# A decoder layer in split f32 on one core: branch B's gate by a seven-product scheme behind v, ua beside the attention stages, branch A's gate whole beside the last heads

## The chip, the core and the metric

The kernel runs on one core of a Trainium2 chip. The metric is the device time of one execution, in microseconds (us). Three runs of the kernel before gave 615.21, 615.33 and 616.19 us, a median of 615.33. The profiles are of one execution each. The engines are called PE (matrix products), PEld (the loads of PE's stationary operand), DVE, ACT and POOL (the three that work on vectors); SP only issues transfers.

## The reference, cut to what matters

One layer, 512 tokens, 1024 channels. A single projection of x gives nine pieces; branch A is a gated mixing of tokens within chunks of 128, branch B an attention with two softmax maps for each of 8 heads.

```python
h = x @ w_in
ua, va, za, qh, kh, vh, zb, ga, gb = jnp.split(h, IN_OFFSETS, axis=-1)

ua = gelu(ua)
va = layer_norm(gelu(va), a_ln_g, a_ln_b)
vc = va.reshape(bn, n_chunks, CHUNK, A_GROUPS, A_GROUP_DIM)
sa = einsum("gts,bnsgc->bntgc", tril(a_w_s), vc) + a_b_s.T[:, :, None]
ya = ua * sa.reshape(bn, s_len, A_WIDTH) * silu(za)

o = diff_attention(rope(qh) * dk ** -0.5, rope(kh), vh, lam)     # 8 heads, two maps each
yb = rms_norm(o, b_subln_g) * (1.0 - lam_init) * silu(zb)

merged = sigmoid(ga) * (ya @ w_branch_a) + sigmoid(gb) * (yb @ w_branch_b)
ple = sigmoid(x @ w_ple_gate) * (p @ w_ple)
return layer_norm(alpha * x + merged @ w_out + ple, ln_g, ln_b)
```

## The kernel before

**Products.** Every f32 operand of a projection is kept as a high part and the remainder (`xh` and `xl` of x, `wh` and `wl` of a weight tile), and one f32 product is three matmuls: high by high, high by low, low by high (`three`, L292). A "product" below is one such matmul, of a stationary 128 x 128 piece by a moving 128 x 512 piece. Weights arrive as raw tiles of 512 KB (128 x 1024, "wr" or "wa"). ACT copies a tile into `wh` (L410), and DVE subtracts that from the raw tile into `wl` (L413).

**Two ways to make 1024 output columns.** The plain way is a group for each 128 features (`feature_group`, L465): eight steps of three products, 24 in all, into one PSUM bank, so 192 for 1024 columns. The other is `quad` (L650), which multiplies the blocks of a 2 x 2 split by seven products of blocks instead of eight: seven steps of 24 products, 168 in all, from sums of blocks of x and sums of blocks of the weights. The sums of weights are made in one of two ways. In a chain (`CHAINS`) the raw tile of a step becomes that of a later step when POOL issues a transfer that adds another weight block to it (`follow`, L385), behind DVE's last read. Or the sums lie ready in DRAM, made earlier by `make_sums` at the points of `READY_MADE`.

**The order.** PE's matmuls are written out in order. `product` (L280) counts them, and `later(n, fn)` puts the work of the other engines n products behind the point at which it is called. So a table of small numbers says beside which product each piece of ACT, DVE, POOL, PE and DMA work is issued; every engine then takes its own instructions in that order. The stages, with their products:

1. kq (96): k and q of heads 0 and 1. Then zb's first pair of feature groups (48), kept in two banks, and v as a quad (168).
2. Three stages of 144: k, q and zb of the next pair of heads (48 each); `attention(p - 1)` for the pair before lies between the products, and `gate_b` puts Silu of zb into `yb`.
3. `attention(3)` beside ua (192, L1050) and the first two groups of za (48, L1079; `HELD`).
4. va as a quad of ready sums (168), then **zq**: the other six groups of za as a narrow quad. It has features on the rows and blocks of three groups, so its 252 matmuls have 256 columns, and its tiles 768 used columns.
5. ga, gb, pg, ple, wb, wa and out. The norm of va (`va_norm`: statistics on DVE, a power on POOL, then `centre` and `shift` of 128 x 1024 on DVE) is issued in zq and ga, by `NORM`; branch A's spatial products (`spatial`, PE, followed by two DVE operations) by `SPATIAL`, 32 products apart.

**A head.** `scores` (L796) takes two of the "sc" banks for a block of queries; DVE reduces each into `p`, ACT takes the exponential, DVE combines the two maps, PE transposes and multiplies by v into the one bank "po" (`values`). The tail of a head is `squares` (DVE and ACT), `norm` (DVE, then POOL's power), `scale` (POOL) and `turned` (PE transposes the head, DVE multiplies the bank by a constant and by `yb`, L888), by `TAIL` products behind the last values. `PERIOD` is the distance of the blocks, `stretch` multiplies it.

Of the kernel before, what the change touches and what calls it, by code (L numbers as in the profile page):

```python
# [21 lines left out]
P = 128  # L22
# [17 lines left out]
EARLY_ASK = ("k", "q", "zb")  # L40
# [6 lines left out]
SWAP = 132  # L47
BEGIN = 14
STRETCH = 1.0
# [4 lines left out]
TAIL = (2, 14, 28, 48)  # L54
NORM = (2, 112, 270, 330)
SPLITS = {'va': ((0, 10), (13, 16)), 'wb': ((4, 7), (13, 16)), 'zq': ((1, 4), (10, 17)), '': ((0, 4), (6, 12))}
BEHIND = (8, 14)
LAST = (7, 11)
GELU = 10
SILU = (20,)  # L60
CENTRE = (12, 24)
SPATIAL = (390, 32)
READY_MADE = {'va': (2, 6, 50, 32, 140, 174, 260, 314), 'wb': (162, 290, 170, 318, 356, 470), 'zq': (320, 430, 434, 538), 'ga': (540, 566), 'gb': (752, 786), 'pg': (612, 745), 'wa': (1500, 1570)}
# [5 lines left out]
FIRST_GATE = 168  # L69
SUMS_OF_X = (60, 75, 84, 84, 150, 152, 174, 179)  # L70
XS = (24, 14, 98, 18)
AUX = (124, 136, 104, 130, 130)
# [4 lines left out]
GOES_ON = ('v', 'gb', 'pg', 'wb', 'wa')  # L77
HELD = 2
BLOCKS = 3
NARROW = 2 * BLOCKS * P  # L80
# [44 lines left out]
def narrow_units(off):  # L125
    return [("n", off + c * BLOCKS * P, kk) for c in range(2) for kk in range(4)]


# [10 lines left out]
PART_READY = {'zq': (0, 2), 'ga': (2,), 'gb': (2,), 'wb': (0, 1, 2), 'pg': (2,), 'wa': (2,)}  # L139
# [6 lines left out]
def plan():  # L146
# [68 lines left out]
def pack(ws):  # L215
    out = np.empty((len(UNITS), P, 1024), np.float32)
    for i, (w, u) in enumerate(UNITS):
# [8 lines left out]
        elif u[0] == "n":  # L226
            _, c, kk = u
            s = a[2 * kk * P:(2 * kk + 2) * P, c:c + BLOCKS * P]
            out[i, :, :NARROW] = s.reshape(2, P, BLOCKS * P).transpose(1, 0, 2).reshape(P, NARROW)
            out[i, :, NARROW:] = 0.0  # L230
# [16 lines left out]
def hybrid_layer(ctx: ExitStack, tc: tile.TileContext, a, out: bass.AP):  # L247
# [79 lines left out]
    def weights(unit, n=1024):  # L327
        return (W[unit] if isinstance(unit, int) else wsd[unit[0]][unit[1], unit[2]])[:, :n]

    def width(name):  # L330

        return NARROW if name == "zq" else 1024

    def make_sums(name, at):

        cols = width(name)
        there = wsd[name][:, :, :, :cols]

        def step(n, what, of, j):
            source = weights((name, of, j) if isinstance(of, int) else MADE_OF[name, of][j], cols)  # L340
# [10 lines left out]
    def load(u, cuts=(0, 1024), first=(sp,)):  # L351
# [15 lines left out]
        cuts = [min(n, width(STEPS[u][0])) for n in cuts]  # L367
# [5 lines left out]
    def follow(u):  # L373
# [6 lines left out]
        else:  # L380
# [3 lines left out]
            n = width(STEPS[u][0])  # L384
            pool.dma_start(out=raw[u][:, :n], in_=weights(STEPS[FOLLOWS[u]][1], n), accum_op=OP.add)  # L385
# [7 lines left out]
    def prep(u, cuts=(0, 1024)):  # L393
        if u < len(STEPS) and u not in split:
            run(load(u))
            h, l = parts_of(u)
            cuts = [min(n, width(STEPS[u][0])) for n in cuts]
# [5 lines left out]
    def spread(u, high=HIGH[0], low=LOW[0]):  # L403
# [3 lines left out]
        h, l = (part[:, :width(STEPS[u][0])] for part in parts_of(u))  # L407

        def high_part():
            act.activation(h, raw[u][:, :width(STEPS[u][0])], AF.Copy)  # L410

        def low_part():
            dve.tensor_tensor(out=l, in0=raw[u][:, :width(STEPS[u][0])], in1=h.bitcast(F32), op=OP.subtract)  # L413
            follow(u)
# [18 lines left out]
    def next_pair(name, i):  # L433
# [7 lines left out]

        pace = BLOCKS / 2 if name == "zq" else 1

        def ask(at, v, fits=lambda chain: True):
            if not pumping and v < len(STEPS) and fits(STEPS[v][2]):
                later(round(at * pace), lambda: run(load(v)))
# [8 lines left out]
        for j, at in enumerate(SPLITS.get(name, SPLITS[""])):  # L455

            at = BEHIND if i == 5 and j and name not in SPLITS else LAST if i == 6 and j else at
            spread(u + 2 + j, *(round(pace * n) for n in at))
# [191 lines left out]
    def quad(name, left, banks, place, done):  # L650
# [4 lines left out]
        if name == "zq":  # L655
            X, Y, Z = ([bank[:, :(2 - t) * 2 * P] for t, bank in enumerate(two)] for two in banks)
        kept = {}

        def keep(key, bank):
            kept[key] = tmp[0](key[0])[:, :bank.shape[-1]]  # L660
# [16 lines left out]
        def after2(t):  # L677
            if goes_on:
                z = place(0, t)
                return done(0, t, tmp[0]("s1")[:, :X[t].shape[-1]] if z is None else z, X[t])  # L680
# [18 lines left out]
        def after4(t):  # L699
            z = place(0, 2 + t)  # L700
            done(0, 2 + t, tmp[0]("z")[:, :Y[t].shape[-1]] if z is None else z, Y[t])
# [3 lines left out]
        for i, (bank, first, after) in enumerate(steps):  # L705
            w = next_pair(name, i)
            for t in range(2):
                if name == "zq":
                    for j, k in ((j, k) for j in range(2 - t) for k in range(4)):
                        h, l = w[k // 2]  # L710
                        m = slice(((k % 2) * BLOCKS + 2 * t + j) * P, ((k % 2) * BLOCKS + 2 * t + j + 1) * P)
                        three(bank[t][:, j * 2 * P:(j + 1) * 2 * P], h[:, m], l[:, m], *left[i](None, k),
                              first and k == j == 0, k == 3, True)
                else:
                    for k in range(4):
                        h, l = w[k // 2]
                        m = slice((k % 2) * T, (k % 2 + 1) * T)
                        three(bank[t], *left[i](t, k), h[:, m], l[:, m], first and k == 0, k == 3, True)
# [63 lines left out]
    def gate_b(p, banks, at):  # L782
        for bank in banks:
            feature_group(bank, "zb", xh, xl)

        def out_of():
            for i, bank in enumerate(banks):
                act.activation(yb[0][:, 2 * p + i, :], bank, AF.Silu)

        later(at, out_of)  # L790


    def attention(p, begin, stretch=1.0):
# [87 lines left out]

        def turned(h):
# [4 lines left out]
            z = yb[0][:, h, :]  # L887
            dve.scalar_tensor_tensor(out=z, in0=tr, scalar=g08[:, 0:1], in1=z, op0=OP.mult, op1=OP.mult)  # L888

        at = begin  # L890
        for hd in range(2):
# [9 lines left out]
            for d, fn in zip(TAIL, (squares, norm, scale, turned)):  # L901
# [76 lines left out]
    gate_b(0, (pbank("tr", 1), pbank("po", 1)), FIRST_GATE)  # L978

    ua = big.tile([P, KT, T], F32, name="ua", tag="U")  # L980

    def ua_out(g, bank):
        act.activation(ua[:, g, :], bank, AF.Copy)

    def ua_groups(groups):
        for g in groups:
            bank = pp()
            feature_group(bank, "ua", xh, xl)
            later(2, ua_out, g, bank)

    yb = []

    def place_yb():
        yb.append(big.tile([P, NH, T], F32, name="yb", tag="Y"))
# [4 lines left out]
    def v_done(c, t, z, source):  # L999
        if source is not z:  # L1000
# [3 lines left out]
    later(FIRST_GATE - 1, place_yb)  # L1004
    quad("v", operands(xh, xl, [of_piece(j) for j in range(4)]),
         ([pp(), pp()], [pbank("sc", 2) for _ in range(2)], [pp(), pbank("tx", 1)]), place_v, v_done)
    sums.clear()
    for name, at in READY_MADE.items():
        make_sums(name, at)
    for p in range(1, 4):  # L1010
# [3 lines left out]
        gate_b(p, (pp(), pp()), GATE)  # L1014
# [35 lines left out]
    ua_groups(range(KT))  # L1050

    def ua_gelu(g):
        act.activation(ua[:, g, :], ua[:, g, :], AF.Gelu)

    def za_groups(groups):
        def gate_a(g, bank):
            sz = bp.tile([P, T], F32, name="sz", tag="sz", bufs=4)

            def silu(source):
                act.activation(sz, source, AF.Silu)  # L1060
# [429 lines left out]
```

## Time and profile before

| | before |
|---|---|
| median of 3 runs | 615.33 us |
| the profiled execution | 615.15 us |
| its span | 613.4 us, so 1.75 us lie outside it |
| mean granted clock of PE | 0.997 |
| instructions | 8568 |
| HBM read, written | 121.05 MB, 32.64 MB: 251 GB/s over the span |

The profile gives busy times by engine, the span in 40 slices, the chain of waits that ended last, groups of instructions by line and tile, and the windows of any stretch. Busy times of neighbouring matmuls overlap, since the matmuls are pipelined; the distance of two starts is what one costs in a stream. A row of the timeline is: start in us, duration in us, engine, line, operation, out<-in, shape, and in brackets the idle time before it with what ended that.

### The profile page before, as it was taken

Reading aid. Unit: us, or ns where it says so; the run is one execution under the profiler, and the core shown is the slowest. Engines: PE = TensorE matmul, PEld = TensorE weight load, DVE = VectorE, ACT = ScalarE, POOL = GpSimd, SP = SyncE. Lnnn points to the kernel's source line nnn. Section 1 sums busy time; section 2 is a strip of 40 time slices with the busy share of each in tenths; the row PEclk is TensorE's granted clock in tenths of the full one; section 3 lists DMA queues with packets and bytes.
Section 4 is the critical chain, followed back from the end, with each engine's and each line's share of the span. In section 5 each row is a group of like instructions: output and inputs, shape, how many; then the busy total and the mean of one; then the engine's idle time right before and its main releaser. Section 6 shows DMA issues by size and latency. Waiting matters only on the chain.

```text
span 613.4 us, 8568 instructions
## 1 busy us (share of the span) xinstructions
PE 605.1 (99%) x3012; PEld 510.1 (83%) x3012; DVE 464.5 (76%) x776; ACT 342.3 (56%) x537; POOL 121.5 (20%) x133
## 2 busy tenths in 40 slices
PE   9999999999999999999999999999999999999995
PEld 6888888888888888888889988888888888888884
DVE  6995677879879865856669878668787887879476
ACT  6656565564555564458656665555676464555310
POOL 1234002332422512220012111131220011110011
PEclk9999999999999999999999999999999999999998
DMA  8689889779697599559897899886989578998002
GB/s 309 221 245 182 251 297 241 261 208 309 240 241 284 186 262 299 126 180 283 258 336 197 217 243 233 251 199 186 291 236 316 172 192 245 243 251 310 30 34 104
DMA packets 45983, 140.62 MB, mean 229 GB/s; under 512 B 6100, under 2 KB 7252, under 8 KB 45588
## 3 DMA queue, kind: packets, MB, share of 16 engines
q1 hardware_dynamic: 35876, 106.38, 48.8%
q0 software_dynamic: 9488, 33.30, 29.9%
q8 instruction: 24, 0.39, 0.3%
q10 hardware_dynamic: 576, 0.39, 0.2%
q14 instruction: 19, 0.16, 0.1%
HBM read 121.05 MB, written 32.64 MB: 251 GB/s over the span
## 4 chain that ended last, share of the span: by engine, by line
PE 99%; DVE 0%; DVEq 0%; issue 0%
PE ps_pp L281 58%; PE ps_sc L281 19%; PE ps_tx L281 9%; PE ps_sc L802 3%; PE ps_po L847 3%; PE ps_tr L836 1%; PE ps_po L281 1%; PE ps_tr L281 1%; PE ps_po L485 1%; PE ps_tr L1173 1%; PE ps_po L1173 1%; PE ps_tx L886 0%; PE ps_po L1360 0%; PE ps_tr L1360 0%; DVE base L1402 0%; DVEq L1486 0%
## 5 line engine op out<-in xcount | busy, mean ns | idle before, releaser
L413 DVE TENSOR_TENSOR wl<-wr,wh 128x1024 fp32r<-128x1024 f32 (+1 forms) x143 | 177.8, 1250 | 39.3 <-ACT wh L410 39.0
L410 ACT ACTIVATE wh<-wr 128x1024 fp32r<-128x1024 f32 (+1 forms) x143 | 146.3, 1033 | 68.4 <-PE ps_pp L281 17.1
L281 PE MATMUL ps_pp<-xh,wh 128*128 128x512 f32 (+1 forms) x276 | 109.6, 398 | 0.0
L281 PE MATMUL ps_pp<-xl,wh 128*128 128x512 f32 (+1 forms) x276 | 107.3, 389 | 0.0
L281 PE MATMUL ps_pp<-xh,wl 128*128 128x512 f32 (+1 forms) x276 | 105.6, 383 | 0.0
L385 POOL DMA_DIRECT2D wr<-in_w x32 | 27.7, 876 | 181.0 <-DVE wl L413 127.0
L815 ACT ACTIVATE p<-p,sth 128x128 f32<-128x128 f32 (+3 forms) x64 | 35.5, 556 | 46.6 <-DVE sth L813 46.5
L281 PEld LDWEIGHTS ps_pp<-xh,wl 128*128 128x128 f32 x276 | 52.2, 189 | 8.8
L281 PEld LDWEIGHTS ps_pp<-xh,wh 128*128 128x128 f32 x276 | 52.3, 190 | 8.5 <-ACT wh L307 0.5
L281 PEld LDWEIGHTS ps_pp<-xl,wh 128*128 128x128 f32 x276 | 52.2, 189 | 8.2 <-DVE xl L308 0.4
L281 PE MATMUL ps_pp<-wh,xl 128*128 128x512 f32 (+1 forms) x144 | 55.4, 384 | 0.0
L281 PE MATMUL ps_pp<-wl,xh 128*128 128x512 f32 (+1 forms) x144 | 55.3, 384 | 0.0
L281 PE MATMUL ps_pp<-wh,xh 128*128 128x512 f32 (+1 forms) x144 | 55.2, 383 | 0.0
L747 POOL TENSOR_TENSOR hl<-m,hl 128x512 fp32r<-128x512 f32 x16 | 25.2, 1637 | 54.3 <-ACT hl L742 54.3
L809 DVE CUSTOM_DVE_ANT_0 p<-ps_sc,mask 128x128 f32<-128x128 f32 (+3 forms) x64 | 30.9, 483 | 6.4 <-PE ps_sc L802 6.3
L281 PE MATMUL ps_sc<-wl,xsh 128*128 128x512 f32 x88 | 34.4, 391 | 0.0
L281 PE MATMUL ps_sc<-wh,xsh 128*128 128x512 f32 x88 | 34.3, 390 | 0.0
L281 PE MATMUL ps_sc<-wh,xsl 128*128 128x512 f32 x88 | 34.2, 389 | 0.0
L281 PEld LDWEIGHTS ps_pp<-wl,xh 128*128 128x128 f32 x144 | 27.1, 188 | 5.3
L281 PEld LDWEIGHTS ps_pp<-wh,xl 128*128 128x128 f32 x144 | 27.1, 188 | 5.2
L281 PEld LDWEIGHTS ps_pp<-wh,xh 128*128 128x128 f32 x144 | 27.1, 188 | 5.2
L281 PE MATMUL ps_pp<-wh,xsl 128*128 128x512 f32 x80 | 31.2, 390 | 0.0
(321 smaller groups left out, 1280.8 us busy)
## 6 DMA issues: line engine op xcount, KB each, us to landing
wr<-in_w SPq DMA_DIRECT2D x81, 512.0 KB, 5.2
wr<-in_w POOLq DMA_DIRECT2D x28, 512.0 KB, 7.1
k<-hl SPq DMA_DIRECT2D x16, 256.0 KB, 5.5
q<-hl SPq DMA_DIRECT2D x16, 256.0 KB, 4.2
ws_va<-in_w POOLq DMA_DIRECT2D x8, 512.0 KB, 10.5
wr<-ws_va SPq DMA_DIRECT2D x8, 512.0 KB, 4.1
wa<-in_w POOLq DMA_DIRECT2D x6, 512.0 KB, 7.1
kx<-hl SPq DMA_DIRECT2D x12, 256.0 KB, 5.6
```

The lines of the kernel that those rows point to most:

```text
L281: pe.matmul(ps, s, m, start=start, stop=stop, skip_group_check=read_within)
L385: pool.dma_start(out=raw[u][:, :n], in_=weights(STEPS[FOLLOWS[u]][1], n), accum_op=OP.add)
L410: act.activation(h, raw[u][:, :width(STEPS[u][0])], AF.Copy)
L413: dve.tensor_tensor(out=l, in0=raw[u][:, :width(STEPS[u][0])], in1=h.bitcast(F32), op=OP.subtract)
L485: pe.matmul(idle, zeros[:, :P], zeros, start=True, stop=True)
L747: pool.tensor_tensor(out=hl[:, 3 - j, :], in0=m[2 * j], in1=hl[:, j, :].bitcast(F32), op=OP.subtract)
L802: pe.matmul(sc[m][:, :n], q[:, m, i * P:(i + 1) * P], kk[:, m, :n], start=o == 0, stop=o == 1)
L809: dve.tensor_tensor_reduce(out=pr[m][:, :n], in0=sc[m][:, :n], in1=mask[:, T - n:], scale=-(DK ** -0.5), scalar=3e38, op0=OP.add, op1=OP.m ...
L815: act.activation(pr[m][:, :n], pr[m][:, :n], AF.Exp, bias=st[:, m:m + 1], scale=-1.0, accum_out=st[:, 2 + m:3 + m])
L836: pe.transpose(tr[:, j * P:(j + 1) * P], ad[:, j * P:(j + 1) * P], ident)
L847: pe.matmul(po[:, i * P:(i + 1) * P], at[:, j * P:(j + 1) * P], v[:, j, h * P:(h + 1) * P], start=j == 0, stop=j == i)
L1173: pe.matmul(sa[:, t * P:(t + 1) * P], va[:, t, g * P:(g + 1) * P], aux[0][:, 0, g, :], start=True, stop=True)
```

## The change

- **zb** is one quad (168 products) right behind v, from the same sums of x. Its seven products end in tokens by features, Silu goes straight into `yb` (tag U). The chains of its weights are as v's.
- **ua** takes zb's place: pair 0 in two banks behind kq, pairs 1 to 3 in the three attention stages (`ua_pair`, Gelu from the bank). It moves from tag U to tag Y.
- **The gate of a head** is multiplied in before the turn: `gated` (DVE, `on` by `yb`) is a new step of the tail, between `scale` and `turned`; ACT then copies the turned bank into `yb`, scaled by the constant. The last head has a tail of its own (`LAST_TAIL`).
- **za** is eight plain groups (192) beside `attention(3)`, whose blocks come closer (`STRETCH` 0.78). Groups 0 to 4 are copied out of their bank and get Silu later (`SILU`), the last three at once. zq, its narrow tiles and all code for them go.
- **va** takes the banks in another order; the four norms of va are issued in ga (`NORM` 174, 224, 276, 326 from va's start), and the spatial products in gb, 17 apart. The points of the ready-made sums, of x's sums and of the norm's constants move: ga takes pg's, pg takes zq's.

```diff
-EARLY_ASK = ("k", "q", "zb")
+EARLY_ASK = ("k", "q", "ua")
-STRETCH = 1.0
+STRETCH = 0.78
 PERIOD = (13, 16, 20, 23)
-TAIL = (2, 14, 28, 48)
-NORM = (2, 112, 270, 330)
+TAIL = (2, 14, 26, 44, 56)
+LAST_TAIL = (2, 10, 20, 32, 42)
+SILU = (122, 5)
+NORM = (174, 224, 276, 326)
-SPATIAL = (390, 32)
+SPATIAL = (194, 17)
...
-GOES_ON = ('v', 'gb', 'pg', 'wb', 'wa')
+GOES_ON = ('v', 'zb', 'gb', 'pg', 'wb', 'wa')
...
     add("kq", "in", [("c", cols, kk) for kk in range(4)])
-    add("zb", "in", feature_units(ZB, 2))
+    add("ua", "in", feature_units(UA, 2))
     quad("v", "in", token_units(VO))
+    quad("zb", "in", token_units(ZB))
     for p in range(1, 4):
         add("k", "in", rope_units(KO, p))
         add("q", "in", rope_units(QO, p))
-        add("zb", "in", feature_units(ZB + 2 * p * P, 2))
-    add("ua", "in", feature_units(UA, KT))
-    add("za", "in", feature_units(ZA, HELD))
+        add("ua", "in", feature_units(UA + 2 * p * P, 2))
+    add("za", "in", feature_units(ZA, KT))
     ready_quad("va", "in", token_units(VA))
-    quad("zq", "in", narrow_units(ZA + HELD * P))
...
+        def gated(h):
+            on, _ = todo["sq", h]
+            dve.tensor_tensor(out=on, in0=on, in1=yb[:, h, :].rearrange("p (i d) -> p i d", i=NT), op=OP.mult)
+
         def turned(h):
...
-            z = yb[0][:, h, :]
-            dve.scalar_tensor_tensor(out=z, in0=tr, scalar=g08[:, 0:1], in1=z, op0=OP.mult, op1=OP.mult)
+            act.activation(yb[:, h, :], tr, AF.Copy, scale=g08[:, 0:1])
...
-            for d, fn in zip(TAIL, (squares, norm, scale, turned)):
+            for d, fn in zip(TAIL if h < NH - 1 else LAST_TAIL, (squares, norm, scale, gated, turned)):
...
+    def zb_done(c, t, z, source):
+        act.activation(yb[:, 4 * c:4 * c + 4, t * P:(t + 1) * P], source.rearrange("p (h d) -> p h d", h=4), AF.Silu)
+
+    one, two = [pp(), pp()], [pp(), pbank("tx", 1)]
+    quad("zb", of_pieces, (two, [pbank("sc", 2) for _ in range(2)], one), lambda c, t: None, zb_done)
...
+    def keep_z(g, bank):
...
+        act.activation(z, bank, AF.Copy)
+        later(SILU[0] + SILU[1] * g - clock[0] + began, gate_a, g, z, z)
+
+    def gate_a(g, z, source):
+        act.activation(z, source, AF.Silu)
+        later(4, times, g, z)
+
+    began = clock[0]
     for g in range(KT):
-        later(GELU + 2 * g, ua_gelu, g)
-    za_groups(range(HELD))
-    flush(8)
+        bank = pp()
+        feature_group(bank, "za", xh, xl)
+        if g < 5:
+            later(2, keep_z, g, bank)
+        else:
+            later(2, gate_a, g, bp.tile([P, T], F32, name="sz", tag="sz", bufs=3), bank)
+    flush(14)
...
-    quad("va", of_x, pairs(False), lambda c, t: va[:, t, c * T:(c + 1) * T], va_done)
     for t in range(NT):
         later(NORM[t], va_norm, t)
+    quad("va", of_x, ([pp(), pp()], [pbank("sc", 2) for _ in range(2)], [pp(), pbank("tx", 1)]),
+         lambda c, t: va[:, t, c * T:(c + 1) * T], va_done)
     for g in range(KT):
         later(SPATIAL[0] + SPATIAL[1] * g, spatial, g)
-    quad("zq", of_x, pairs(True), lambda c, t: None, za_done)
```

The order of the instructions at three places follows. First PE's queue at the end of va. Before, va's last matmuls stand ahead of zq's first:

```order
L281 MATMUL ps_pp<-wh,xh 128x512
L281 MATMUL ps_pp<-wl,xh 128x512
L281 MATMUL ps_pp<-wh,xl 128x512
L281 MATMUL ps_pp<-xh,wh 128x256
L281 MATMUL ps_pp<-xl,wh 128x256
L281 MATMUL ps_pp<-xh,wl 128x256
```

After, on the same engine at the same place, ga's first matmuls follow va's last:

```order
L268 MATMUL ps_sc<-wh,xh 128x512
L268 MATMUL ps_sc<-wl,xh 128x512
L268 MATMUL ps_sc<-wh,xl 128x512
L268 MATMUL ps_pp<-wh,xh 128x512
L268 MATMUL ps_pp<-wl,xh 128x512
L268 MATMUL ps_pp<-wh,xl 128x512
```

The 252 matmuls of 256 columns are gone from this place; the columns that they made stand in the stage before va.

Second, DVE's queue behind the last values of the last head (`on` is the head, `xt` a sum of x for va, `ss` and `ok` the sums of squares). Before:

```order
L856 TENSOR_TENSOR on<-ps_po,r0h 128x512
L858 TENSOR_SCALAR on<-on 128x512
L413 TENSOR_TENSOR wl<-wr_2640,wh 128x1024
L1043 TENSOR_TENSOR xt<-xt 128x2x256
L868 TENSOR_REDUCE ss<-sq 128x4
L869 TENSOR_SCALAR ok<-ss 128x4
L870 TENSOR_SCALAR ss<-ss 128x4
L872 TENSOR_SCALAR ss<-ss 128x4
L1043 TENSOR_TENSOR xt<-xt 128x2x256
L413 TENSOR_TENSOR wl<-wr_2711,wh 128x1024
L1043 TENSOR_TENSOR xt<-xt 128x2x256
L888 SCALAR_TENSOR_TENSOR yb<-ps_tr,g_123,yb 128x512
```

After, on the same engine behind the same values (`ua` by `sz` is branch A's gate):

```order
L824 TENSOR_TENSOR on<-ps_po,r0h 128x512
L826 TENSOR_SCALAR on<-on 128x512
L392 TENSOR_TENSOR wl<-wr_2877,wh 128x1024
L1006 TENSOR_TENSOR xt<-xt 128x2x256
L836 TENSOR_REDUCE ss<-sq 128x4
L837 TENSOR_SCALAR ok<-ss 128x4
L838 TENSOR_SCALAR ss<-ss 128x4
L840 TENSOR_SCALAR ss<-ss 128x4
L1014 TENSOR_TENSOR ua<-ua,sz 128x512
L1006 TENSOR_TENSOR xt<-xt 128x2x256
L392 TENSOR_TENSOR wl<-wr_2962,wh 128x1024
L852 TENSOR_TENSOR on<-on,yb 128x512
```

The gate's multiply now stands on DVE ahead of PE's transposes, where before a multiply stood behind them, and a product of branch A's gate lies in the tail.

Third, DVE's queue in ga, at the two blocks that are made from the "sc" banks (`s_` tiles). Before:

```order
L666 TENSOR_TENSOR s_3842<-ps_sc,s_3842 128x512
L666 TENSOR_TENSOR s_3864<-ps_sc,s_3864 128x512
L413 TENSOR_TENSOR wl<-wr_3296,wh 128x1024
L666 TENSOR_TENSOR s_3758<-s_3758,ps_pp 128x512
L413 TENSOR_TENSOR wl<-wr_3374,wh 128x1024
L1179 TENSOR_TENSOR y<-ps_po,aux 128x512
```

After, on the same engine at the same two blocks:

```order
L1106 BN_STATS vst<-va 128x6 x2
L1093 BN_AGGR mv<-vst 128x2
L1094 TENSOR_SCALAR mv<-mv 128x1
L392 TENSOR_TENSOR wl<-wr_3476,wh 128x1024
L641 TENSOR_TENSOR s_3673<-ps_sc,s_3673 128x512
L1110 SCALAR_TENSOR_TENSOR va<-va,mv,a_ln_g 128x1024
L641 TENSOR_TENSOR s_3696<-ps_sc,s_3696 128x512
L392 TENSOR_TENSOR wl<-wr_3277,wh 128x1024
L1114 SCALAR_TENSOR_TENSOR va<-va,rs,a_ln_b 128x1024
L641 TENSOR_TENSOR s_3589<-s_3589,ps_pp 128x512
```

One of va's four norms now stands among the blocks and the weight subtractions of ga's middle; before, the first spatial product's operations came there and the norms stood earlier.

More of the change, by code (lines that the diff above doesn't have):

```diff
@@ L383, in follow @@
                 home[FOLLOWS[u]] = home.pop(u)
-            n = width(STEPS[u][0])
-            pool.dma_start(out=raw[u][:, :n], in_=weights(STEPS[FOLLOWS[u]][1], n), accum_op=OP.add)
+            pool.dma_start(out=raw[u], in_=weights(STEPS[FOLLOWS[u]][1]), accum_op=OP.add)
     def parts_of(u):
@@ L457, in next_pair @@
             at = BEHIND if i == 5 and j and name not in SPLITS else LAST if i == 6 and j else at
-            spread(u + 2 + j, *(round(pace * n) for n in at))
+            spread(u + 2 + j, *at)
         return split.pop(u), split.pop(u + 1)
@@ L654, in quad @@
         X, Y, Z = banks
-        if name == "zq":
-            X, Y, Z = ([bank[:, :(2 - t) * 2 * P] for t, bank in enumerate(two)] for two in banks)
         kept = {}
         def keep(key, bank):
-            kept[key] = tmp[0](key[0])[:, :bank.shape[-1]]
+            kept[key] = tmp[0](key[0])
             act.activation(kept[key], bank, AF.Copy)
@@ L707, in quad @@
             for t in range(2):
[L708 to L718, printed above, removed]
+                for k in range(4):
+                    h, l = w[k // 2]
+                    m = slice((k % 2) * T, (k % 2 + 1) * T)
+                    three(bank[t], *left[i](t, k), h[:, m], l[:, m], first and k == 0, k == 3, True)
                 if after:
@@ L977, in hybrid_layer @@
     rope("q", 0, first_kq[2:], TURN_Q, STACK)
[L978 to L994, printed above, removed]
+    first_ua = ua_pair(0, (pbank("tr", 1), pbank("po", 1)))
     def place_v(c, t):
@@ L1013, in hybrid_layer @@
         rope("q", p)
-        gate_b(p, (pp(), pp()), GATE)
+        later(GATE, ua_pair(p, (pp(), pp())))
     attention(3, BEGIN, STRETCH)
```

105 lines of the change are left out of this document (35 added, 70 removed).

## The prediction

> **What bounds the kernel now.** I read the engine table, the slices and the chain of waits first.
>
> ```profile
> PE 605.1 (99%) x3012; PEld 510.1 (83%) x3012; DVE 464.5 (76%) x776; ACT 342.3 (56%) x537; POOL 121.5 (20%) x133
> PE   9999999999999999999999999999999999999995
> PEclk9999999999999999999999999999999999999998
> PE 99%; DVE 0%; DVEq 0%; issue 0%
> ```
>
> TensorE (PE) is busy for 605.1 us of the span of 613.4, in every slice but the last. Its granted clock is in the top tenth until the last slice, and the chain that ended last is 99% PE. So the time is the sum of the matmuls' own time, and a change is worth the matmuls that it takes out, less the waits it makes. What a matmul costs I read from the starts in PE's timeline at three stage borders: va's first, zq's first, ga's first.
>
> ```profile
> 281.36 0.39 PE L281 MATMUL ps_pp<-wh,xh 128*128 128x512 f32 x1
> 319.44 0.28 PE L281 MATMUL ps_pp<-xh,wh 128*128 128x256 f32 x1
> 349.67 0.40 PE L281 MATMUL ps_pp<-wh,xh 128*128 128x512 f32 x1
> ```
>
> va holds 168 matmuls of 512 columns in 319.44 - 281.36 = 38.08 us, **0.2267 us** each. zq holds 252 of 256 columns in 349.67 - 319.44 = 30.23 us, **0.1200 us** each. The printed durations (0.39, 0.28) overlap, and only the distance of the starts counts. Then the windows by stage; the columns are PE, its weight loads, DVE, ACT and POOL busy, the clock, the DMA share and GB/s.
>
> ```profile
> 42.00:76.00 34.00, 34.00 (x152) 28.15 (x151) 22.60 (x28) 21.00 (x27) 7.68 (x8) 1.00 0.91 222
> 122.00:168.00 46.00, 46.00 (x249) 39.11 (x246) 38.45 (x98) 25.70 (x57) 16.02 (x15) 1.00 0.81 253
> 214.00:281.00 67.00, 67.00 (x350) 56.71 (x349) 42.01 (x108) 38.88 (x77) 15.01 (x17) 1.00 0.78 215
> 319.40:349.70 30.30, 30.30 (x254) 30.26 (x254) 25.83 (x35) 20.13 (x30) 5.24 (x8) 1.00 0.82 228
> 349.70:388.00 38.30, 38.30 (x175) 31.84 (x174) 30.08 (x36) 23.07 (x30) 7.93 (x9) 1.00 0.92 234
> ```
>
> They are v, an attention stage, the last attention stage, zq and ga. PE idles in none, though DVE reaches 38.45/46.00 = 84% in an attention stage and 25.83/30.30 = 85% in zq. That is the level known to be harmless.
>
> **The sum of the matmuls.** zb goes from 8 groups of 24 products (192) to one seven-product quad (168): -24 of 512 columns. za goes from two groups held (48) to eight (192): +144. zq's 252 go. ua keeps its 192. So +120 x 0.2267 = +27.20, and -252 x 0.1200 = -30.23: **-3.03 us**. Both prices are elapsed time between starts, so nothing hidden is left to come out of them.
>
> The Trainium skill has another price: "TensorE: Matmul & The Clock Gate", section "Wait — 56ns, not 53.3ns?", gives N / 2.4 + about 2.5 ns for warm back-to-back matmuls. That is 215.7 and 109.2 ns, and the sum would be 120 x 0.2157 - 252 x 0.1092 = -1.63 us, an estimate from that page. The trace's 227 and 120 ns speak against it on both sizes.
>
> **Weights.** zq's half-filled tiles become full ones.
>
> ```profile
> L413 DVE TENSOR_TENSOR wl<-wr,wh 128x768 fp32r<-128x768 f32 x14 | 13.3, 953 | 3.3 <-ACT wh L410 3.3
> L413 DVE TENSOR_TENSOR wl<-wr,wh 128x1024 fp32r<-128x1024 f32 (+1 forms) x143 | 177.8, 1250 | 39.3 <-ACT wh L410 39.0
> ```
>
> The number of tiles that are split stays at 151; 14 subtractions take 1.25 instead of 0.95 us: +4.2 us on DVE, spread over the first half, beside PE. Nothing on the path.
>
> **zb's quad** needs the raw tile of one step to become the next one's by an accumulating transfer, as in v.
>
> ```profile
> 55.93 0.85 POOL L385 DMA_DIRECT2D wa<-in_w  x1 [2.79 <-DVE wl L413]
> 57.78 0.85 POOL L385 DMA_DIRECT2D wa<-in_w  x1 [1.01 <-DVE wl L413]
> wr<-in_w SPq DMA_DIRECT2D x81, 512.0 KB, 5.2
> wa<-in_w POOLq DMA_DIRECT2D x6, 512.0 KB, 7.1
> ```
>
> There are six more of these on POOL's queue, issued by the same rule as v's six, behind DVE's last read of the tile. v ran so with PE busy 34.00 of 34.00 us at a DMA share of 0.91. I take **0**. The nearest bad end is one tile that lands late by the difference of the two kinds of transfer, 7.1 - 5.2 = 1.9 us: range 0 to 1.9. In the other direction nothing can be gained, since PE did not wait here.
>
> **The gate in front of the turn.** Each head gains a DVE multiply by yb before PE's transposes; the multiply of the bank behind them (L888) becomes a copy on ACT. For a head in the middle I read where POOL's scale, DVE and PE stand.
>
> ```profile
> 210.66 1.04 POOL L880 TENSOR_TENSOR on<-on,f 128x512 f32<-128x512 f32 x1
> 212.33 0.75 DVE L827 SCALAR_TENSOR_TENSOR p<-p,rho,p 128x512 f32<-128x512 f32 x1
> 213.45 0.39 PE L886 MATMUL ps_tx<-ident,on 128*128 128x128 f32 x2
> 214.09 0.75 DVE L888 SCALAR_TENSOR_TENSOR yb<-ps_tx,g,yb 128x512 f32<-128x512 f32 x1 [1.01 <-PE ps_tx L886]
> ```
>
> The scale ends at 211.70, 1.75 us before the transposes at 213.45. The new multiply's turn comes 12 products, or 12 x 0.2267 = 2.7 us, ahead of them; the chain between is one operation of 0.75 behind at most one or two of that size. I take **0**; uncovered it would be 0.75 for each of 7 heads, 5.2 us. On DVE itself the multiply takes the place of L888.
>
> **The last head** is the tight one, since the end of the stage is its chain.
>
> ```profile
> 266.36 1.05 PE L847 MATMUL ps_po<-v,at 128*128 128x128 f32 x8
> 267.51 0.69 DVE L856 TENSOR_TENSOR on<-ps_po,r0h 128x512 f32<-128x512 f32 x1 [4.98 <-PE ps_po L847]
> 268.23 0.43 DVE L858 TENSOR_SCALAR on<-on 128x512 f32<-128x512 f32 x1
> 268.58 1.22 DVE L413 TENSOR_TENSOR wl<-wr,wh 128x1024 fp32r<-128x1024 f32 x1
> ...
> 270.31 0.68 DVE L868 TENSOR_REDUCE ss<-sq 128x4 f32<-128x512 f32 x1
> ...
> 271.68 1.41 POOL L873 TENSOR_TENSOR f<-ss,mhalf 128x4 f32<-128x4 f32 x1 [15.56 <-DVE ss L872]
> 273.17 0.22 POOL L874 TENSOR_TENSOR f<-f,ok 128x4 f32<-128x4 f32 x1
> 273.47 1.36 POOL L880 TENSOR_TENSOR on<-on,f 128x512 f32<-128x512 f32 x1
> 278.15 0.60 PE L886 MATMUL ps_tr<-ident,on 128*128 128x128 f32 x4
> ```
>
> From the start of the last values' last matmuls (about 267.0, in the row that ends at 267.41) to the scale's end at 274.83 are 7.8 us, and the transposes came 3.3 us later. Now the multiply (0.69) and a handover of some 0.1 make it 8.6; between the two points stand 39 products and the turn of the last values, about 39 x 0.2267 + 0.2 = 9.0 us. Margin **0.4 us**, so cost 0. Here, though, DVE has the products of ua with za's gate (eight of 0.69, two before) in the same stretch: one of them that falls ahead of the reduction takes the margin and 0.3 us more. I take **+0.2** for this and for all small waits together; range 0 to 1.25, one weight subtraction.
>
> The stage shrinks from 240 products to 192. Its own attention matmuls are 67.00 - 240 x 0.2267 = 12.6 us, so it will last 192 x 0.2267 + 12.6 = 56.1. DVE's work is 42.01 + 6 x 0.69 less two subtractions (2.5) = 43.7, or 78%, below the 84% above.
>
> **The norm of va** now lies whole in ga: before, two of the four were in zq.
>
> ```profile
> L1156 DVE BATCH_NORM_STATS2 vst<-va 128x6 f32<-128x512 f32 x8 | 5.1, 682 | 0.0
> L1160 DVE SCALAR_TENSOR_TENSOR va<-va,mv,a_ln_g 128x1024 f32<-128x1024 f32 x4 | 5.1, 1278 | 0.0
> L1164 DVE SCALAR_TENSOR_TENSOR va<-va,rs,a_ln_b 128x1024 f32<-128x1024 f32 x4 | 5.1, 1277 | 0.0
> ```
>
> One is 2 x 0.68 + 1.28 + 1.28 = 3.9 us. ga's DVE goes from 30.08 to about 30.08 + 2 x 3.9 = 37.9, less the one pair of branch A's spatial products that moves to gb (1.4): **36.5 of 38.1, 96%**. No stretch of the old kernel is so full. Weights are split some 20 products, 4.5 us, ahead of their use; behind a centre or shift and a block this leaves about 0.7 us at the narrowest (four operations, 1.23 + 0.69 + 1.28 + 0.69 = 3.9). So I still take 0, with 0 to 1.3 as range (one operation more ahead). The spatial products 17 instead of 32 apart put two DVE operations (1.4) and 1.3 weight splits into 3.9 us of gb: 77%, harmless.
>
> **Sum.** 615.15 (the profiled run; 613.4 of it the span, and 0.18 below the median of 615.33) - 3.03 + 0.2 = **612.3**.
>
> **Rivals.**
> A. *DVE is late in ga or in the last stage.* For: 96% and a margin of 0.4. Against: nowhere above did an 84% stage stop PE, and DVE may run ahead of its due points. Two places of up to 1.25 us, less the 0.2 counted, with the centre at 1.7: **614.0** (613 to 616).
>
> B. *The short matmuls were worth only half a long one.* 252 x 0.1133 = 28.56 us would be their own time, and the other 1.67 us of zq's 30.23 a wait for weights: the loads are busy 30.26 of 30.30, and the splitting engines may have caught up there. Without that pause the wait comes back in another stage, and the swap frees 28.56 - 27.20 = 1.36 us: **613.8**. Against: PE itself is busy 30.30 of 30.30 there, and va and ga run for 38 us each with no such pause. (The skill's page above stands for this one, with its 1.63.)
>
> C. *Slower: score banks.* The last two heads' blocks begin after 10, 13, 16, 18 products instead of 13, 16, 20, 23, and have two score banks, each freed by a DVE reduction.
>
> ```profile
> L809 DVE CUSTOM_DVE_ANT_0 p<-ps_sc,mask 128x128 f32<-128x128 f32 (+3 forms) x64 | 30.9, 483 | 6.4 <-PE ps_sc L802 6.3
> ```
>
> Ten products are 2.27 us, two reductions 0.97, so 1.3 us of other DVE work may stand ahead. A subtraction with a gate product (1.25 + 0.69 = 1.94) exceeds that by 0.64; at seven block changes this is 4.5 us: 612.3 + 4.5 = **616.8**. It decides once that pair stands ahead of nearly every block. Against: at 78% it will at a few.
>
> D. That the change does not do what it says is out: the order of the instructions shows zb's quad, za's 192 and no zq.
>
> **How the numbers follow.** The measurement tells about 0.2% apart, 1.23 us: faster is below 614.1, slower above 616.6. Forecast 0.70 (611.5 to 613.1, all faster). A 0.18, half on either side of 614.1. B 0.05, faster. C 0.06, slower. 0.01 for the rest, same. Faster 0.70 + 0.09 + 0.05 = 0.84, same 0.10, slower 0.06. The range 611.5 to 614.6 leaves out C, a third of A and a few hundredths of the forecast's own ends.
>
> **What would show it.** va's first matmul should stand at 281.36 + 27.2 = 308.6, ga's at 349.67 - 3.0 = 346.6, and the stages from gb on should last what they did. A wait of PE named for DVE in ga or at the last head's transposes (PE's own gap above 0.2 us) shows A; PE's busy time in the last stage falling under 99% with score banks as the releaser shows C; a quad's 168 matmuls far from 38.1 us shows B. I am wrong if zb's quad waits for weights: then a gap stands on PE in the stage after v.

## The result, and the profile after

The changed kernel takes 611.6 us (median of 4 runs, 611.03 to 612.3) against 615.27 for the kernel before: ratio **0.9938**, 95% interval 0.9921 to 0.9955. That is 3.7 us less; the interval's ends are 2.8 and 4.9 us. The forecast was 612.3, a change of 3.0 to 2.8 us: the right sign, but less than the measured size. The low end of the range was 611.5; the median lies 0.1 above it, and two of the four runs (611.03 and 611.46) lie below it. The profiled run of the changed kernel took 611.03 us, its fastest, with a span of 609.3.

The page of the changed kernel, in the parts shown of the one before:

```profile
span 609.3 us, 8273 instructions
PE 601.1 (99%) x2880; PEld 501.9 (82%) x2880; DVE 466.3 (77%) x770; ACT 345.9 (57%) x537; POOL 125.1 (21%) x133
PE   9999999999999999999999999999999999999995
PE 98%; DVE 1%; DMA 1%; DVEq 0%; issue 0%
PE ps_po L462 <- DVE zeros L459: 1.3, 1, 1.3
PE ps_pp L268 <- DVE xl L295: 0.2, 1, 0.2
```

The last two lines are all of PE's waits: one engine, line and reason, then us, times, longest. Both lie in the first 6 us. Nothing in zb's quad, in the attention stages, at va or in ga made PE wait. The starts of PE's matmuls at the stage borders are these: zb's first, the first attention stage's, the last attention stage's, va's and ga's.

```profile
75.73 0.39 PE L268 MATMUL ps_sc<-wh,xh 128*128 128x512 f32 x1
113.81 0.39 PE L268 MATMUL ps_pp<-xh,wh 128*128 128x512 f32 x1
247.68 0.48 PE L268 MATMUL ps_pp<-xh,wh 128*128 128x512 f32 x1
307.28 0.60 PE L858 MATMUL ps_tr<-ident,on 128*128 128x128 f32 x4
307.63 0.48 PE L268 MATMUL ps_sc<-wh,xh 128*128 128x512 f32 x1
345.85 0.39 PE L268 MATMUL ps_pp<-wh,xh 128*128 128x512 f32 x1
```

(The row at 307.28 is the last head's turn, which stands just ahead of va.) The first product of the last attention stage before, and the last product of the program, before and after:

```profile
210.26 0.48 PE L281 MATMUL ps_pp<-xh,wh 128*128 128x512 f32 x1
606.07 0.28 PE L281 MATMUL ps_pp<-wh,xl 128*128 128x256 f32 x1
602.26 0.28 PE L268 MATMUL ps_pp<-wh,xl 128*128 128x256 f32 x1
```

zb's quad takes 113.81 - 75.73 = 38.08 us, as v and va did. Stage by stage, from the first product of each to that of the next, both profiled runs:

| stage | before, us | after, us | difference | forecast |
|---|---|---|---|---|
| kq, from its first product | 22.76 | 22.30 | -0.46 | 0 |
| the pair behind it, and v | 48.96 | 48.96 | 0 | 0 |
| zb's quad | none | 38.08 | +38.08 | +38.08 |
| three attention stages | 134.08 | 133.87 | -0.21 | 0 |
| last attention stage (240, 192 products) | 71.10 | 59.95 | -11.15 | -10.88 |
| va | 38.08 | 38.21 | +0.13 | 0 |
| zq | 30.23 | none | -30.23 | -30.23 |
| ga, gb and pg | 121.52 | 121.50 | -0.02 | 0 |
| ple, wb, wa and out's products | 134.86 | 134.91 | +0.05 | 0 |
| from the last product to the end | 7.38 | 7.06 | -0.32 | 0 |

With 0.01 at the start they sum to -4.12, the difference of the two profiled runs (615.15 and 611.03). The three large terms are -3.03 by their products; as measured they make -3.30, because the last attention stage lost 0.27 more than 48 products. What the forecast lacks is -0.46 at the start, -0.48 in the attention stages (-0.21 and -0.27) and -0.32 at the end; what it had too much is 0.2 for small waits.

Two rows need a word. ga, gb and pg kept their sum but not their lengths: ga lost 0.93 us, gb gained 1.81 and pg lost 0.90, because one of branch A's eight spatial products lay in ga and one in pg before, and all lie in gb now. And the +0.13 of va lies in its first step, 307.63 to 307.95 in PE's timeline, right behind the last head's turn.

The -0.46 at the start can be read from the first products. Before, and after:

```profile
5.10 0.80 PE L281 MATMUL ps_pp<-xl,wh 128*128 128x512 f32 x1
5.69 0.59 PE L281 MATMUL ps_pp<-xh,wl 128*128 128x512 f32 x1
6.12 0.40 PE L281 MATMUL ps_pp<-xh,wh 128*128 128x512 f32 x1
```

```profile
5.11 0.50 PE L268 MATMUL ps_pp<-xl,wh 128*128 128x512 f32 x1 [0.16 <-DVE xl L295]
5.45 0.39 PE L268 MATMUL ps_pp<-xh,wl 128*128 128x512 f32 x1
5.68 0.39 PE L268 MATMUL ps_pp<-xh,wh 128*128 128x512 f32 x1
```

The two steps take 0.59 and 0.43 us before, 0.34 and 0.23 after: 0.45 of the 0.46. The steps of 0.59 and 0.43 come from PE's clock, which is not yet at full speed there: in the traces' record of the granted clock, it gets there at 6.10 us in the first and at 3.97 us in the second.

The two places that the prediction called tight are ga, shown by its window (after, in the columns that the prediction names), and the last head's chain.

```profile
345.90:383.90 38.00, 38.00 (x169) 31.48 (x168) 33.74 (x43) 23.26 (x29) 9.99 (x10) 1.00 0.89 234
298.61 0.69 DVE L824 TENSOR_TENSOR on<-ps_po,r0h 128x512 f32<-128x512 f32 x1 [0.18 <-PE ps_po L815]
...
305.24 1.04 POOL L848 TENSOR_TENSOR on<-on,f 128x512 f32<-128x512 f32 x1
306.31 0.69 DVE L852 TENSOR_TENSOR on<-on,yb 128x512 f32<-128x512 f32 x1 [1.22 <-POOL on L848]
```

ga's DVE is busy 33.74 of 38.00 us, 89% and not 96%: the last norm ends in gb (its centre and shift are due 170 and 182 products behind ga's first), and the durations of neighbours, which I had added up, overlap by some 0.1 us each. The gate of the last head ends at 307.00, and PE's transposes start at 307.28: the margin is 0.3 us, where 0.4 was worked out.

### The profile page after: what moved, and what is told of

The parts are those of the page before. It is cut to its first block, busy times and chain, and to the rows that moved or that the text cites. A ratio compares the mean times of both kernels' runs of the same rounds, so it can differ in the third digit from the quotient of the medians.

```text
span 609.3 us, 8273 instructions
## 1 busy us (share of the span) xinstructions
PE 601.1 (99%) x2880; PEld 501.9 (82%) x2880; DVE 466.3 (77%) x770; ACT 345.9 (57%) x537; POOL 125.1 (21%) x133
## 4 chain that ended last, share of the span: by engine, by line
PE 98%; DVE 1%; DMA 1%; DVEq 0%; issue 0%
PE ps_pp L268 56%; PE ps_sc L268 22%; PE ps_tx L268 9%; PE ps_sc L770 3%; PE ps_po L815 3%; PE ps_tr L804 1%; PE ps_po L268 1%; PE ps_tr L268 1%; PE ps_tr L1123 1%; PE ps_po L1123 1%; DMA xr<-in_xT 1%; PE ps_tx L858 1%; PE ps_tr L1309 0%; PE ps_po L1309 0%; DVE base L1351 0%; DVE xl L295 0%
## 5 line engine op out<-in xcount | busy, mean ns | idle before, releaser
L392 DVE TENSOR_TENSOR wl<-wr,wh 128x1024 fp32r<-128x1024 f32 x133 | 166.4, 1259 | 39.8 <-ACT wh L389 39.7
L389 ACT ACTIVATE wh<-wr 128x1024 fp32r<-128x1024 f32 x133 | 139.2, 1054 | 73.3 <-PE ps_pp L268 18.0
L268 PE MATMUL ps_pp<-xh,wh 128*128 128x512 f32 x232 | 94.0, 406 | 0.0
L268 PE MATMUL ps_pp<-xl,wh 128*128 128x512 f32 x232 | 92.7, 400 | 0.2 <-DVE xl L295 0.2
L268 PE MATMUL ps_pp<-xh,wl 128*128 128x512 f32 x232 | 91.8, 396 | 0.0
L365 POOL DMA_DIRECT2D wr<-in_w x30 | 25.8, 873 | 155.8 <-DVE wl L392 152.8
L268 PEld LDWEIGHTS ps_pp<-xl,wh 128*128 128x128 f32 x232 | 43.7, 188 | 7.9 <-DVE xl L295 0.5
L268 PEld LDWEIGHTS ps_pp<-xh,wh 128*128 128x128 f32 x232 | 43.7, 188 | 7.9 <-ACT wh L294 0.5
L268 PEld LDWEIGHTS ps_pp<-xh,wl 128*128 128x128 f32 x232 | 43.7, 188 | 7.7
L268 PE MATMUL ps_pp<-wh,xsl 128*128 128x512 f32 x72 | 28.1, 390 | 0.0
```

The lines of the kernel that those rows point to most:

```text
L268: pe.matmul(ps, s, m, start=start, stop=stop, skip_group_check=read_within)
L365: pool.dma_start(out=raw[u], in_=weights(STEPS[FOLLOWS[u]][1]), accum_op=OP.add)
L389: act.activation(h, raw[u], AF.Copy)
L392: dve.tensor_tensor(out=l, in0=raw[u], in1=h.bitcast(F32), op=OP.subtract)
```

## The experiments

Stage lengths below are read as in the table. All runs stood beside the kernel before on the same chip, and the times are medians.

**The two kernels again** (no edit), for the scatter. Of the kernel before:

> The kernel before, unchanged, against itself. Ratio 1.000; its interval shows what a ratio of this case can tell. Theory P (the time is the count of products times 0.2267 and the count of short matmuls times 0.1200; whatever is left of the difference is scatter between executions): kq's first stage, which was 0.46 us shorter in the profile of the changed kernel, comes out anywhere between 22.3 and 22.8 us. Theory S (the changed kernel is also systematically quicker at the start and the tail): 22.8 again, and 10.2 us behind the last product.

615.97 us (11 runs, 614.8 to 617.24) against 615.42: ratio 1.0008, 0.9999 to 1.0017. The profiled one was the slowest, and shows what scatters: kq's stage 23.18 us (more than the 22.8 that either theory gave), gb 44.49 instead of 43.52, wa 40.73 instead of 40.03, and waits that the first profile did not have. From the last product to the end it took 7.36 us; the 10.2 us of the expectation is not that distance.

```profile
PE ps_pp L281 <- ACT wh L307: 0.6, 1, 0.6
PE ps_sc L281 <- DVE wl L413: 0.4, 1, 0.4
PE ps_tx L281 <- ACT s L661: 0.4, 1, 0.4
PE ps_pp L281 <- DVE xl L308: 0.2, 1, 0.2
```

The first and last are at the start, the second is a weight tile in wa that came late, and the third lies in gb. Of the changed kernel:

> The changed kernel again, for a narrower interval than 0.9921 to 0.9955. Theory P: nearer to 615.15 - 3.03 - about 0.3 for shorter attention stages, a ratio of 0.9945 to 0.995, and the first stage of kq not the same 22.3 us as in its first profile. Theory S: 0.9935 to 0.994, and 22.3 us again.

611.84 us (5 runs), ratio 0.994, 0.9928 to 0.9953. kq's stage took 22.83 us here, and the end 7.01. So the start's -0.46 was scatter: over all fourteen traces of the study kq's stage lies between 22.30 and 23.46 us, with either kernel (22.37 in one of the kernel before with closer blocks), and full clock begins between 3.97 and 7.21 us. The attention stages (133.87 and 59.95) and the end came out the same again: they are not scatter. Theory P holds for the start, theory S for the end; the ratio, 0.994, is the upper end of what S gave.

**zb in plain groups.**

```diff
-    quad("zb", "in", token_units(ZB))
+    add("zb", "in", token_units(ZB))
...
-    quad("zb", of_pieces, (two, [pbank("sc", 2) for _ in range(2)], one), lambda c, t: None, zb_done)
+    for c in range(2):
+        banks = [pp(), pp(), pbank("sc", 2), pbank("sc", 2)] if c else first_four
+        token_chunk(banks, "zb", xh, xl)
+        for t, bank in enumerate(banks):
+            later(2, zb_done, c, t, None, bank)
```

> The changed kernel with zb in plain groups of tokens (192 products) where its quad of 168 stood. Theory P: 24 products more, 24 x 0.2267 = +5.44 us against the changed kernel, so 616.5 to 617.5, ratio to the kernel before about 1.002; the stages behind keep their lengths. Rival: the quad had waits of its own or gave shorter attention stages (its chain of transfers is gone here); then the difference is under 4.5 us or over 6.5 us.

618.15 us, ratio 1.0042 (1.0027 to 1.0058): 6.3 us above the changed kernel, and 0.65 above the range that theory P gave.

```profile
76.63 0.39 PE L268 MATMUL ps_sc<-wh,xh 128*128 128x512 f32 x1
120.15 0.39 PE L268 MATMUL ps_pp<-xh,wh 128*128 128x512 f32 x1
```

zb's stage took 120.15 - 76.63 = 43.52 us instead of 38.08, **+5.44**, to the hundredth the 24 products. The rest is elsewhere: the last attention stage 60.35 (+0.40), the end 7.38 (+0.35). So the quad's part is as forecast, and had no waits of its own.

**za in plain groups, in the kernel before.**

```diff
-HELD = 2
+HELD = 8
-NORM = (2, 112, 270, 330)
+NORM = (174, 224, 276, 326)
-SPATIAL = (390, 32)
+SPATIAL = (194, 17)
...
-    quad("zq", of_x, pairs(True), lambda c, t: None, za_done)
```

> The kernel before with za alone changed: eight plain groups behind ua, no narrow quad, va's norm in ga; zb and the gate of the heads as before. Theory P: 144 products for 252 short ones, 32.64 - 30.24 = +2.40 us, so 617.7, ratio 1.004. Rival B of the prediction (a short matmul is worth half a long one, 28.56 us, and zq's other 1.67 us were a wait that comes back elsewhere): +4.1 us, 619.4.

618.12 us, ratio 1.0043 (1.0029 to 1.0056), +2.7.

```profile
210.75 0.48 PE L280 MATMUL ps_pp<-xh,wh 128*128 128x512 f32 x1
314.48 0.39 PE L280 MATMUL ps_sc<-wh,xh 128*128 128x512 f32 x1
```

The last attention stage with za took 103.74 us (from unrounded starts) instead of 71.10, +32.64; zq's 30.23 are gone: **+2.41**. I put the other 0.3 down to scatter of the kind above. In the profiled run, the slowest, kq's stage took 23.33 us and wa's 40.87 instead of 40.03, with this wait:

```profile
PE ps_pp L280 <- DVE wl L412: 0.5, 1, 0.5
```

(The kernel before, run again, had 40.73 in the same stage.) The quad's -5.44 and za's +2.41 make -3.03. Rival B falls: it asked for 1.7 us of waits beyond that, and the stages that took zq's and za's place have none.

**The last head's turn earlier.**

```diff
-LAST_TAIL = (2, 10, 20, 32, 42)
+LAST_TAIL = (2, 10, 20, 30, 34)
```

> The last head's gate and turn 2 and 8 products earlier. Theory P (the chain from the last values to the gated head is what the margin of 0.3 us in the changed kernel's profile measures: the gate ends at 307.00, the transposes start at 307.30): 8 products are 1.81 us, so PE waits 1.81 - 0.30 = 1.5 us for DVE's gate in front of the transposes, and the time is 1.5 us above the changed kernel's, about 613.2. Rival (the chain runs as late as it is asked to and has room): under 0.5 us of wait, time as the changed kernel.

612.44 us, ratio 0.995 (0.9934 to 0.9967). PE does wait for the gate:

```profile
306.10 0.39 PE L268 MATMUL ps_pp<-xh,wh 128*128 128x512 f32 x1
307.33 0.63 PE L858 MATMUL ps_tr<-ident,on 128*128 128x128 f32 x4 [0.85 <-DVE on L852]
```

0.85 us, where I expected 1.5. I had counted 8 products; but the stage's products end 39 behind the last values, and the turn is issued there and not at 42. So the edit moved it by 5 products, 1.13 us, and 1.13 - 0.30 = 0.83 is what the margin gives. The stage is 61.08 instead of 59.95, and va behind it 38.09 instead of 38.21: its first step no longer follows a turn. Both together grew by 1.01 us. The chain is what binds here, and the margin is real.

**The blocks closer still.**

```diff
-STRETCH = 0.78
+STRETCH = 0.6
```

> STRETCH 0.6 instead of 0.78: the last two heads' blocks after 8, 10, 12, 14 products. Rival C of the prediction (two score banks, each freed by a DVE reduction, decide once some 1.3 us of other DVE work stands ahead; with 8 products, 1.81 us, that falls to 0.85): PE waits at most of the seven block changes, the stage is over 2 us longer than 59.95 us. Theory P (DVE at 78% of the stage keeps up): under 0.5 us longer, time within 0.5 us of the changed kernel. I expect between: some waits, 0.5 to 2 us.

617.43 us, ratio 1.0025 (1.0012 to 1.0039): slower than the kernel before. The stage took 66.38 us, 6.4 more. But no wait is at a score bank. PE's waits, the stretch of PE behind the longest, and one wait of DVE's:

```profile
PE ps_tr L858 <- DVE on L852: 3.0, 1, 3.0
PE ps_po L815 <- DVE on L824: 1.4, 1, 1.4
...
307.92 1.09 PE L858 MATMUL ps_tr<-ident,on 128*128 128x128 f32 x4 [3.03 <-DVE on L852]
308.65 0.78 PE L268 MATMUL ps_pp<-xh,wh 128*128 128x512 f32 x1
309.23 0.63 PE L268 MATMUL ps_pp<-xl,wh 128*128 128x512 f32 x1
309.66 0.63 PE L268 MATMUL ps_pp<-xh,wl 128*128 128x512 f32 x1
310.08 0.63 PE L268 MATMUL ps_pp<-xh,wh 128*128 128x512 f32 x1
...
DVE on L824 <- PE ps_tx L858: 2.9, 1, 2.9
```

`on`, the tile of a head's output, has one buffer (`squares` asks for it in a pool with one buffer a name). DVE cannot begin the next head's until PE has turned this one. The turn stands at 56 products behind a head's last values and `squares` at 2, so two heads must lie 54 products apart. At 0.78 they lie 72 x 0.78 = 56 apart, at 0.6 only 43: DVE waits 2.9 us, the last head's gate comes late, and PE waits 3.0. The 1.4 us are at another place, the one bank `po`: PE cannot begin the last head's values there until DVE has read those of the head before. The two waits, and 1.3 us of slow products behind the longer one (last section), make 5.7 of the 6.4 us. Rival C's place was wrong: no wait at a score bank shows at 0.6. By the table the buffer of `on` would begin to bind at a stretch of 54 / 72 = 0.75; no run between 0.6 and 0.78 tested that.

**More DVE work in ga**, one and two operations in each of va's norms:

```diff
         def centre():
+            for c in range(1):
+                same = z[:, c * T:(c + 1) * T]
+                dve.tensor_tensor(out=same, in0=same, in1=same, op=OP.max)
```

> One more DVE operation of 128x512 (0.69 us, an in-place maximum of a value with itself) in each of va's four norms, 2.8 us in all. DVE in ga goes from the 33.7 us measured to 36.5 of 38.1, the 96% that the prediction gave for the changed kernel. Theory P: PE does not wait at 96% either (ga 38.1 us, under 0.3 us more). Rival A (full DVE stops PE): 0.5 to 1.5 us more, PE waiting for DVE's wl or blocks in ga.

> Two more such operations in each norm, 5.5 us in all: 39.3 us of DVE for a stage of 38.1. Theory P and rival A agree that PE has to wait here, unless work slips into gb, whose DVE is busy 78%: 0.5 to 2 us more, at weights (wl) or at the first spatial product, which waits for the last norm. No wait at all would mean that DVE's busy time is no bound of this stage and the 96% of the prediction no danger.

One: 611.45 us (2 runs, ratio 0.9934, 0.9913 to 0.9955), ga 38.08, no wait. Two: 612.39 us (4 runs, ratio 0.9951, 0.9934 to 0.9968), ga 38.44, so 0.36 us of stop. The windows of ga, one and two:

```profile
345.90:383.90 38.00, 38.00 (x169) 31.48 (x168) 35.76 (x46) 23.29 (x30) 9.79 (x10) 1.00 0.86 233
```

```profile
345.90:383.90 38.00, 37.93 (x168) 31.09 (x167) 36.69 (x47) 23.23 (x29) 9.71 (x9) 1.00 0.86 227
```

35.76 of 38.00 (94%) does not stop PE, 36.69 (97%) begins to. Of the 5.5 us added, 3 fell into ga and the rest ran later. So the prediction's fear for a DVE at 96% was of the right size, but the changed kernel is at 89%, and has room for one operation in each norm; the second costs 0.36 us.

**Fewer breaks of PE's stream**, a version that might beat both:

```diff
-VALUES = (35, 45, 44, 45)
+VALUES = (35, 46, 43, 46)
```

> The changed kernel with VALUES (35, 46, 43, 46) instead of (35, 45, 44, 45): three of a head's products by v now stand right at a transpose or a score block, so PE's stream of long products is broken 96 times instead of 117. Theory M (the shorter attention stages of the changed kernel come from fewer breaks, each with a late start of 0.088 us behind it): 21 x 0.09 = 1.9 us less than the changed kernel, about 609.8. Rival (a merged block costs nearly what its two parts cost, 0.909 against 0.712 + 0.118 us, and most close pairs share one late start already): under 0.5 us less, or more time where a bank or a copy comes late.

and with `TAIL = (2, 14, 25, 41, 53)` as well:

> As the run before, and TAIL (2, 14, 25, 41, 53): a head's turn stands right at a transpose of the next head too, 93 breaks. Theory M: some 0.3 us less than the run before. Rival: no less; and the gate, now 3 products nearer to POOL's scale, may wait.

612.03 us (ratio 0.9934, 0.9921 to 0.9948) and 612.22 (0.9939, 0.9927 to 0.9952): no better than the changed kernel. The first attention stage became 0.38 us shorter (41.97), the next two stayed (45.77 and 45.79), and the last grew by 0.7 (60.68, 60.74), 0.3 of it a wait at the bank of the products by v:

```profile
PE ps_po L815 <- DVE on L824: 0.3, 1, 0.3
```

Theory M falls. In the second stage the distances from each product to the next matmul sum to 34.21 us, where the changed kernel has 34.79: fewer late starts. But those from attention's and the turns' matmuls grew from 10.97 to 11.56. What a merged break saves behind it, the longer block takes back; only the first stage kept its gain.

**Two small loads more on SP.**

```diff
-        for i, n in enumerate(("q1", "k1", "q2", "k2")):
+        for i, n in ((0, "q1"), (1, "k1"), *enumerate(("q1", "k1", "q2", "k2"))):
```

> The changed kernel with two of its smallest loads (128x64) issued twice on SP: 253 transfers on SP instead of 251. In the traces so far the close of the program takes 3.05 us behind DVE's last operation where SP issues 251 transfers (remainder 3 of 8) and 3.41 us where it issues 253 or 261 (remainder 5), whatever else differs. Theory Q (SP works off a fixed list of ten waits of 63 ns at the end, and the place of the last output's wait in it goes by the count of transfers modulo 8): the close takes 3.41 us here, 0.36 more, and the time is some 0.4 us above the changed kernel. Rival (the shorter close belongs to something else in the changed kernel): 3.05 us as before.

612.03 us (3 runs, ratio 0.9953, 0.993 to 0.9976). The last product of this run, whose span is 610.1 us:

```profile
602.69 0.28 PE L268 MATMUL ps_pp<-wh,xl 128*128 128x256 f32 x1
```

From there to the end are 7.38 us instead of 7.01 to 7.06, with the other stages behind kq as in the changed kernel to 0.03 us. So the -0.32 at the end belongs to the number of transfers, 251 on SP after and 261 before. In all fourteen traces the end takes 7.00 to 7.06 us with 251 and 7.36 to 7.38 with 253 or 261. That it goes by the count modulo 8, as theory Q says, is not shown: only two remainders were run.

**Closer blocks alone, in the kernel before.**

```diff
-STRETCH = 1.0
+STRETCH = 0.78
```

> The kernel before with the last two heads' blocks as close as in the changed kernel (STRETCH 0.78), all else left. Theory R (the 0.27 us that the last attention stage lost beyond its products comes from where the blocks fall among the products): the stage goes from 71.10 to about 70.8 us, the rest stays. Rival (it comes from the gate's new place or from za's groups): 71.1 us, or longer with new waits.

614.96 us, ratio 0.9999 (0.9988 to 1.001): too small a change for the time to show. The last attention stage took 70.92 us instead of the 71.10 of both traces of the kernel before: 0.18 of the 0.27 go with where the blocks fall among the products. Theory R holds for the larger part, from one trace.

## Why the prediction was right in kind and short in size

- **The step that failed: the terms beside the counted products.** The sum had +0.2 for small waits and, without a reason given, nothing for what stands between and behind the products. No wait came at the places that the +0.2 was for. The attention stages lost 0.48 us beyond their products, and the end 0.32. With these, and +0.17 of va and the small rest, the sum is -3.03 - 0.48 - 0.32 + 0.17 = -3.66, which is the measured 3.7. The cause of the 0.32 is shown (the number of SP's transfers), that of 0.18 of the 0.48 by one run (where the blocks fall); the other 0.30 stays open.
- **The price of a product and the sum.** Right to 0.01 us, in both parts taken alone (+5.44 and +2.41). The Trainium skill's price ("TensorE: Matmul & The Clock Gate", section "Wait — 56ns, not 53.3ns?"), 215.7 ns for 512 columns, would have made 24 products 5.18 us, an estimate from that page; measured are 5.44, so the row of the trace decides: 226.7 ns.
- **zb's chain of transfers at 0.** Right: 38.08 us, no wait.
- **The gate in front of the turn at 0.** Right for the seven heads in the middle. For the last head the margin of 0.4 was measured as 0.3, and the run with the earlier turn shows that it is a true bound.
- **The norm in ga at 0.** Right, but not at the load worked out: DVE is at 89%, not 96%. With two operations more in each norm, at 97%, PE begins to stop.
- **The length of the last attention stage.** The prediction took a window of 67.00 us for the whole stage and forecast 56.1. The stage began at 210.26 and lasted 71.10, and it now lasts 59.95. The sum used only the difference of 48 products, so by luck the slip did not reach it; DVE's share of 78% came out too (46.85 of 59.90 us). va's first product came at 307.63 instead of 308.6, ga's at 345.85 instead of 346.6.
- **"The stages from gb on should last what they did."** Wrong for gb (+1.81) and pg (-0.90); with ga's -0.93 the three cancel.
- **The range.** Its low end, 0.8 below the forecast, left little room for such gains and for the scatter at the start, which alone spans 1.2 us between executions.
- **Rivals.** A did not come about, B is refuted by za alone, and C did not come about at 0.78; at 0.6 the blocks do stop PE, but not at the score banks.

Open stay the 0.10 us that the second and third attention stage each became shorter (in the second, 0.08 of it lies in the distances from product to next matmul, 34.87 and 34.79 us for the 144), the remaining 0.09 of the last stage, and its 0.40 more when zb is plain.

## What to carry to other kernels

Where one engine is busy all the time, the difference of two starts in a stage without waits prices each kind of its instructions, and a sum over the counts forecasts what they cost: here to 0.01 us in the two parts that were run alone. Look behind them for what is not a count: where a tile has one buffer, work out how far apart its users must stay (54 products here, by the table of distances) before moving them closer. And a range needs the scatter of the run's start and the fixed cost at its end, even where the change touches neither.

## What the hardware showed that I had not expected

- **The end of this program has a length that goes with the number of transfers.** Behind DVE's last operation SP works off ten waits in a fixed order, some 61 ns apart where nothing holds them up. With 261 or 253 transfers issued by SP (remainder 5 of 8) the one for the last output is the third, done at 2.08 us, and seven more follow, so that the span ends at 3.4 us. With 251 (remainder 3) it is the ninth, one follows, and the span ends at 3.03 to 3.09. This is read from the semaphore events of the traces; no other remainder was run.
- **A long wait of PE can cost more than its length.** Behind the 3.03 us wait in the run with stretch 0.6, the next products start 427 ns apart (309.23, 309.66, 310.08) instead of 227, so that six products take 1.3 us more in all, and the window of these shows the granted clock (the third number from the end) at half. In the trace's record of the clock the half speed lasts from 307.77 to 311.18, 3.41 us.

```profile
308.60:311.20 2.60, 2.60 (x8) 2.12 (x8) 1.51 (x2) 0.69 (x1) 0.00 (x0) 0.50 0.39 109
```

  The Trainium skill's page on the clock gate ("TensorE: Matmul & The Clock Gate", section "Wait — 56ns, not 53.3ns?") gives 426.7 ns for 512 columns on a cold (throttled) array, and the starts agree. Behind the 0.85 us wait of the run with the earlier turn, and behind the 1.35 us wait at `po` in the run with stretch 0.6, the clock stayed at 1.00. The 0.43 us between two first products of the kernel before, ahead of its full clock at 6.10 us, is the same slow pace.
